# Attention in a diffusion step: rotary partners copied by DMA between partitions, the rotation on VectorE over 128 partitions one unit later

## The chip, the cores and the metric

One core of a Trainium2 chip runs the whole program. The metric is the device time of one execution in microseconds. TensorE (PE in the profile, its weight loads PEld) multiplies, VectorE (DVE), ScalarE (ACT) and GpSimd (POOL) do the elementwise work, and SyncE (SP) issues most of the DMA transfers. Each engine works through its own instructions one after the other.

## The reference

One inference step of a network of two layers over 128 context tokens and 512 latent tokens with 1024 features, in float32. Each layer has a SwiGLU block, a mixer, and a second SwiGLU block; the mixer of the first layer is a convolution with a gated unit, that of the second is attention. The change lies in that attention. Cut to what matters:

```
def rope_half(xp, ang):                       # xp: (..., 2F), cos and sin by position and feature
    a, b = xp[..., :F], xp[..., F:]
    return concatenate([a * cos - b * sin, b * cos + a * sin])

def axial_rope(x, ang_r, ang_c):              # 64 features of a head: 32 turn by the row, 32 by the column
    return concatenate([rope_half(x[..., :32], ang_r), rope_half(x[..., 32:], ang_c)])

qs, ks_, vs = split_qkv(hs @ attn_w_qkv[j])   # latent: 16 query heads, 4 key heads, 64 features each
qs, ks_ = axial_rope(qs, ...), axial_rope(ks_, ...)
ys = latent_attention(qs, ks_, vs, k_ctx, v_ctx, sink) @ attn_w_o[j]
```

The context tokens have attention of their own, without rotation. Latent queries see a window of 128 positions to either side and 128 cached context keys, with a learned sink in the softmax.

## The kernel before

**Layout.** Features lie on the 128 partitions, tokens along the free dimension: 128 context tokens and then 512 latent ones. All products are made in three float32r products of a high and a low part (`mm3`): a value is split into a high part, copied by ScalarE, and the rest, subtracted by VectorE. So each weight block costs a DMA, a ScalarE copy and a VectorE subtraction (`wload_ahead`, lines 184 to 213) before TensorE can use it, and so does each activation.

**The projections** (lines 1354 to 1392 and 1552 to 1555). Output block i of `wqkv` holds 128 features: blocks 0 to 7 are two query heads each, 8 and 9 two key heads each. A unit is one block for the 384 tokens of group GA or the 256 of GB: 24 matmuls in one PSUM bank, and an evacuation by ScalarE into `Q` (block i of the buffer `Y`) or `ks`. Blocks 0 to 3, 8 and 9 go in pairs for GA, with the making of `h` woven in; then GB of the keys and of blocks 0 to 3, and blocks 4 to 7 for both groups. `weights(i)` fetches a block where it is called, 4 to 7 within this run; buffers for raw weights are three, for split pairs six.

**The rotation** (`rope`, lines 1257 to 1272). The features are ordered so that a feature's partner lies 32 partitions away in the same 64. For a block of 512 latent tokens VectorE makes four products over 32 partitions each, partner times sine into a buffer `tmp` (four of these); POOL multiplies the block by the cosine in place over 128 partitions; VectorE adds. The sum is held back until the next rotation has begun (`last_rope`). Block 6 is taken otherwise: ScalarE copies the partners, and POOL makes both products. The keys go in two halves of 256 tokens, since 128 cached keys lie between them.

**The order.** Tensor, vector, scalar and POOL instructions are kept in the order of the code by a wrapper, `InOrder` (lines 61 to 78), and so all of them bear line 71 in the profile. DMAs on `nc.sync` are not wrapped; a planner places them. Keys and blocks 0 to 4 are rotated between the projections' units, each some units behind its evacuation. Between them lie `split_prompt` and `split_keys`, which split the keys for the scores, and the weights `wv` of the values (line 1387).

**The scores.** `prepare(t)` splits the 128 queries of token block t; t = 0 is the context, which isn't rotated. It can run when unit (7, GA) is evacuated. The first scores (`scores(0)`) follow unit (7, GB) on TensorE. The loop over m (lines 1571 to 1601) has eight steps per token block: scores two steps ahead, five pieces of value projection while m < 8, transposes of the probabilities, the exponentials, and six items of `leftover()`: the rotations of blocks 5 to 7 and `prepare(1)`, all during t = 0. Later `prepare(t)` casts on POOL.

Of the kernel before, what the change touches and what calls it, by code (L numbers as in the profile page):

```python
# [10 lines left out]
AF = mybir.ActivationFunctionType  # L11
ALU = mybir.AluOpType
AX = mybir.AxisListType

P = 128
# [5 lines left out]
NS = 512  # L21
# [68 lines left out]
class Builder:  # L90
# [1163 lines left out]
    def att_weight(self, i):  # L1254
        return ("qk", i), self.a["wqkv"][i], KC

    def rope(self, s, pos, on_act=False):


        nc, V = self.nc, self.nc.vector  # L1260
        t = self.tmp(pos.stop - pos.start)
        shaped = lambda u: u if len(s.shape) == 2 else u.rearrange("p (t q) -> p t q", q=P)
        sin, cos, t = (shaped(u) for u in (self.rsin[:, pos], self.rcos[:, pos], t))
        sides = [(slice(o, o + 32), slice(o ^ 32, (o ^ 32) + 32)) for o in range(0, P, 32)]
        first = [lambda: nc.pool.tensor_tensor(out=s, in0=s, in1=cos, op=ALU.mult)]

        if on_act:
            swap = [lambda r=r, q=q: nc.scalar.activation(out=t[r], in_=s[q], func=AF.Copy) for r, q in sides]
            first.append(lambda: nc.pool.tensor_tensor(out=t, in0=t, in1=sin, op=ALU.mult))
        else:  # L1270
            swap = [lambda r=r, q=q: V.tensor_tensor(out=t[r], in0=s[q], in1=sin[q], op=ALU.mult) for r, q in sides]
        return swap + first, lambda: V.tensor_tensor(out=s, in0=s, in1=t, op=ALU.subtract if on_act else ALU.add)

    def attention(self, h, lead, nxt, fetches):
        nc, a = self.nc, self.a
        V = nc.vector
        wts = {}
        Q = self.Y.rearrange("p (t i q) -> p t i q", i=KC, q=P)


        ks = [self.act() for _ in range(2)]
# [3 lines left out]
        def weights(i):  # L1285
            if i not in wts:
                wts[i] = self.take(*self.att_weight(i))
            return wts[i]

        def evac(ps, i, g):  # L1290
            if i < 8:
                nc.scalar.activation(out=Q[:, g[0] // P:g[1] // P, i, :], in_=ps.rearrange("p (t q) -> p t q", q=P),
                                     func=AF.Copy, scale=-0.125)
            elif g == GA:
                n = i - 8
                nc.scalar.activation(out=kpr[:, n * P:n * P + P], in_=ps[:, :P], func=AF.Copy)
                nc.scalar.activation(out=ks[n][:, 0:2 * P], in_=ps[:, P:], func=AF.Copy)
            else:
                nc.scalar.activation(out=ks[i - 8][:, 3 * P:], in_=ps, func=AF.Copy)

        def unit(i, g):
            evac(self.proj(weights(i), h, g), i, g)
# [2 lines left out]
            for ps, n in zip(self.proj2([weights(i), weights(j)], h, g, inserts), (i, j)):  # L1305
                evac(ps, n, g)

        last_rope = []

        def rope(s, pos, on_act=False):  # L1310

            ops = []

            def first():
                f, add = self.rope(s, pos, on_act)
                ops.extend(f)
                ops.pop(0)()
                last_rope.append(add)

            yield first  # L1320
            for _ in range(5 if on_act else 4):
                yield lambda: ops.pop(0)()
            yield lambda: last_rope.pop(0)() if len(last_rope) > 1 else None

        def rope_q(i, on_act=False):
            return rope(Q[:, 1:, i, :], slice(0, NS), on_act)

        def rope_k(n):
            return [f for half in range(2) for f in rope(ks[n][:, 3 * P * half:3 * P * half + 2 * P],
                                                         slice(2 * P * half, 2 * P * half + 2 * P))]  # L1330

        def run(*ops):
            for u in ops:
                for f in u:
                    f()
# [4 lines left out]
        def split_prompt():  # L1340
            for e in range(2):
                r = SIDE[e]
                for o in SIDE:
                    nc.scalar.activation(out=dup0[o, :, e, :], in_=pr(kpr[r]), func=AF.Copy)
                V.tensor_tensor(out=pr(kl0[r]), in0=pr(kpr[r]), in1=dup0[r, :, e, :].bitcast(F32), op=ALU.subtract)

        def split_keys(c):
            for e in range(2):
                r = SIDE[e]
                for o in SIDE:  # L1350
                    nc.scalar.activation(out=kst[2 * c + e][o], in_=ks[c][r], func=AF.Copy)
                V.tensor_tensor(out=kl[c][r], in0=ks[c][r], in1=kst[2 * c + e][r].bitcast(F32), op=ALU.subtract)
# [11 lines left out]
        kst = [self.act(F32R, lo=n % 2) for n in range(4)]  # L1364
        kl = [self.act(F32R, lo=True) for n in range(2)]
        weights(4)
        unit(0, GB)
        run(rope_k(0))
        unit(1, GB)
        weights(5)  # L1370
        run(rope_k(1))
        unit(2, GB)
        split_prompt()
        run(rope_q(0))
        unit(3, GB)
        weights(6)
        run(rope_q(1))
        unit(4, GA)
        split_keys(0)
        unit(4, GB)  # L1380
        weights(7)
        run(rope_q(2))
        unit(5, GA)
        split_keys(1)
        unit(5, GB)

        wv = [p for kk in range(2) for p in self.wload(a["wqkvv"][kk], 4, 256)]
        vs = self.vtok
        run(rope_q(3))
        unit(6, GA)  # L1390
        run(rope_q(4))
        unit(6, GB)

        def v_tile(t):

            ps = self.ps()
            for k in range(KC):
                yield lambda k=k: self.mm3(ps[:, :256], tuple(u[:, t * P:(t + 1) * P] for u in h[k]), wv[k],
                                           k == 0, k == KC - 1)
            yield lambda: nc.scalar.activation(out=vs[t], in_=ps[:, :256], func=AF.Copy)  # L1400
            if t == 0:
                nc.sync.dma_start(out=a["o_v"], in_=vs[0])
# [3 lines left out]
        qs, sc, st, pts, pos, op, ess, later = ({} for _ in range(8))  # L1406
# [9 lines left out]
        def prepare(t, engine=None):  # L1416

            qs[t] = self.wpair(D)
            st[t] = tuple(self.sm(16, n) for n in ("nmx", "ssum"))
            ops = [], []  # L1420
            for hf in range(2):
                q, *u = (u[:, hf * 512:hf * 512 + 512] for u in (self.y[t], *qs[t]))
                for r, o, v in zip(SIDE, SIDE[::-1], u):
                    if engine is None:
                        ops[0].append(lambda q=q, r=r, v=v: nc.scalar.activation(out=v[r], in_=q[r], func=AF.Copy))
                    else:
                        ops[0].append(lambda q=q, r=r, v=v: engine.tensor_copy(v[r], q[r]))
                    ops[1].append(lambda q=q, r=r, o=o, v=v: V.tensor_tensor(
                        out=v[o], in0=q[r], in1=v[r].bitcast(F32), op=ALU.subtract))
            return ops  # L1430
# [113 lines left out]
        load, parts = self.first_products(a["wo"], [0, 1], xsel, pieces=2, small=True)  # L1544
# [5 lines left out]
        n = len(steps)  # L1550
# [2 lines left out]
        up, low = prepare(0)  # L1553
        run(up, low)
        unit(7, GB)
        scores(0)()
        scores(1)()
        run(v_tile(0))

        def leftover():  # L1560

            for i in (5, 6, 7):
                yield from rope_q(i, i == 6)
            yield lambda: last_rope.pop(0)()
            up, low = prepare(1)
            yield from up
            yield from low
# [3 lines left out]
        for m in range(n + 4):  # L1571
            if m % 8 == 5 and m < n - 12:
                slow = [f for u in prepare(m // 8 + 2, nc.pool) for f in u]
            if m == n - 11:
                slow = load(0) + load(1)
            if m == n - 5:
                ops, res = self.wload_ahead(a["wo"][2], 2, 512, 2, True)
                wa.append(res)
                slow += ops
            if m == n - 1:  # L1580
                fill = parts
            exp = scores(m + 2) if m + 2 < n else None
            for _ in range(5 if m < 8 else 1):
                if fill:
                    fill.pop(0)()
            if m < n:
                transposes(m)
            if exp:
                exp()
            for _ in range(6):  # L1590
                next(extra, lambda: None)()
            if m != n - 11 and slow:
                slow.pop(0)()
            if 0 < m <= n and m % 2 == 0:
                for k, f in enumerate(values(m - 1)):
                    later.setdefault(m + (1, 2, 2, 3)[k], []).append(f)
            for f in later.pop(m, ()):
                f()
            if m == 8:
                while fill:  # L1600
                    fill.pop(0)()
# [371 lines left out]
```

## Time and profile before

| | |
|---|---|
| median of 3 runs | 2314.23 us (2311.72 to 2314.33) |
| the profiled execution | 2313.76 us |
| its span, first to last instruction | 2312.0 us |
| mean granted TensorE clock | 0.989 |
| busy: PE, PEld, DVE, ACT, POOL | 97%, 88%, 72%, 45%, 12% |
| rotation on POOL, 13 products | 1636.75 to 1702.6 us |
| scores begin | 1678.32 us |

All times are microseconds from the start of the span. A row of a timeline gives start, length, engine, line, operation, and the tile written and read, then the idle time of the engine before it and what ended that. The waits sum up such idle times: who waited for whom, how often, the longest. A group of instructions gives count, busy time and the mean in nanoseconds of one, then the idle time before them. A table by stage gives for each stretch the busy time of each engine, the granted clock (1.00 is full), the DMA share and GB/s.

### The profile page before, as it was taken

How to read it: one execution, taken by the hardware profiler on the slowest of the kernel's cores; microseconds unless marked ns; L12 is line 12 of the kernel's file. 1: busy time of each engine (PE TensorE's matmuls, PEld its weight loads, DVE VectorE, ACT ScalarE, POOL GpSimd, SP SyncE). 2: the span in 40 equal slices, each digit the busy share in tenths (PEclk: the TensorE clock that was granted, in tenths of full speed). 3: DMA queues.
4: the chain of work that ended last, by engine and by line, in shares of the span. 5: the costliest groups of instructions: out<-in, count | busy, mean ns of one | idle time of the engine just before them, and what ended most of it. 6: DMA issues, size and time to landing. Idle time of an engine off the chain costs nothing.

```text
span 2312.0 us, 35269 instructions
## 1 busy us (share of the span) xinstructions
PE 2253.7 (97%) x13692; PEld 2042.7 (88%) x13692; DVE 1658.4 (72%) x2758; ACT 1045.7 (45%) x1845; POOL 282.9 (12%) x377
## 2 busy tenths in 40 slices
PE   9999999999999999999998999999989999999998
PEld 7979898989889898989898989898866797989897
DVE  5688776877867786867777777786788678636366
ACT  5223343553165443434554434345558564434342
POOL 1000101021002111010011010102121021111100
PEclk9999999999999999999999999999989999999999
DMA  8564867542224577776636686864000345665644
GB/s 299 175 233 151 211 186 205 169 174 90 76 101 126 183 195 188 200 187 170 226 112 209 174 211 181 210 182 178 28 21 10 128 122 187 166 140 152 140 126 181
DMA packets 137672, 370.08 MB, mean 160 GB/s; under 512 B 14464, under 2 KB 16384, under 8 KB 136736
## 3 DMA queue, kind: packets, MB, share of 16 engines
q1 hardware_dynamic: 103952, 299.93, 38.0%
q0 software_dynamic: 33552, 67.90, 16.8%
q8 instruction: 107, 1.75, 0.3%
q14 instruction: 61, 0.50, 0.1%
HBM read 322.90 MB, written 42.25 MB: 158 GB/s over the span
## 4 chain that ended last, share of the span: by engine, by line
PE 71%; DVE 14%; DMA 6%; issue 5%; ACT 4%; POOL 1%; DVEq 0%; SPq 0%; ACTq 0%; POOLq 0%
PE ps L71 71%; DVE tmp L71 4%; DMA raw<-wmodT 4%; DVE scr L71 3%; DVE w L71 3%; ACT w L71 2%; DVE raw L71 1%; DMA rawx<-ws 1%; DVE act L71 1%; ACT tmp L71 1%; ACT act L71 1%; DVE Y L71 0%; ACT sum L71 0%; DVE sum L71 0%; DMA raw<-wu 0%
## 5 line engine op out<-in xcount | busy, mean ns | idle before, releaser
L71 PE MATMUL ps<-act,w 128*128 128x320 f32 (+6 forms) x6024 | 918.7, 320 | 25.2 <-DVE w L71 14.1
L71 PEld LDWEIGHTS ps<-act,w 128*128 128x128 f32 (+1 forms) x6024 | 849.2, 185 | 58.8 <-DVE w L71 18.7
L71 PE MATMUL ps<-w,act 128*128 128x512 f32 (+1 forms) x3480 | 785.3, 385 | 4.6 <-ACT tmp L71 3.1
L71 PEld LDWEIGHTS ps<-w,act 128*128 128x128 f32 x3480 | 627.0, 189 | 141.0 <-ACT tmp L71 3.5
L71 DVE TENSOR_TENSOR w<-raw,w 128x1024 fp32r<-128x1024 f32 (+1 forms) x340 | 410.7, 1220 | 205.3 <-ACT w L71 198.1
L71 PE MATMUL ps<-sum,w 128*128 128x320 f32 x3168 | 486.6, 312 | 14.4 <-ACT tmp L71 14.3
L71 PEld LDWEIGHTS ps<-sum,w 128*128 128x128 f32 x3168 | 474.2, 190 | 18.9 <-ACT tmp L71 18.9
L71 ACT ACTIVATE w<-raw 128x1024 fp32r<-128x1024 f32 (+1 forms) x340 | 350.6, 1047 | 194.8 <-DVE raw L71 97.5
L71 ACT ACTIVATE tmp<-ps 128x320 f32<-128x320 f32 (+4 forms) x450 | 209.4, 469 | 377.8 <-PE ps L71 310.2
L71 DVE CUSTOM_DVE_ANT_0 scr<-raw,cbc 128x1024 bf16<-128x1024 f32 x256 | 313.4, 1224 | 88.4 <-DMA raw<-wmodT 83.1
L71 ACT ACTIVATE act<-tmp 128x256 fp32r<-128x256 f32 (+4 forms) x238 | 114.8, 497 | 364.8 <-DVE tmp L71 364.7
L71 DVE TENSOR_TENSOR act<-tmp,act 128x256 fp32r<-128x256 f32 (+4 forms) x240 | 124.8, 528 | 116.9 <-ACT act L71 115.8
L911 POOL DMA_DIRECT2D ys<-tmp x120 | 91.3, 774 | 660.3 <-ACT tmp L71 650.5
L689 POOL DMA_DIRECT2D rawx<-ws x66 | 79.9, 1211 | 654.1 <-DMA rawx<-ws 194.4
L71 DVE TENSOR_TENSOR w<-rawx,w 128x1024 fp32r<-128x1024 f32 x66 | 80.8, 1224 | 28.7 <-ACT w L71 27.1
L71 DVE TENSOR_TENSOR tmp<-ps,tmp 128x320 f32<-128x320 f32 x132 | 64.0, 485 | 24.4 <-PE ps L71 21.4
L71 DVE TENSOR_TENSOR tmp<-tmp,tmp 128x640 f32<-128x640 f32 (+1 forms) x98 | 68.8, 715 | 6.4
L71 ACT ACTIVATE tmp<-ps,sh,G 128x256 f32<-128x256 f32 (+1 forms) x120 | 60.3, 525 | 22.7 <-PE ps L71 22.6
L71 ACT ACTIVATE w<-rawx 128x1024 fp32r<-128x1024 f32 x66 | 69.3, 1051 | 0.0
L71 DVE TENSOR_TENSOR tmp<-tmp,ps 128x320 f32<-128x320 f32 (+2 forms) x110 | 52.7, 479 | 18.0 <-ACT tmp L71 17.2
L71 ACT ACTIVATE tmp<-Y 128x1024 bf16<-128x1024 f32 (+2 forms) x39 | 35.1, 901 | 57.3 <-DVE Y L71 57.2
L71 ACT ACTIVATE Y<-X 128x1024 f32<-128x1024 f32 x30 | 31.8, 1058 | 54.7 <-DVE X L71 50.6
(165 smaller groups left out, 1281.9 us busy)
## 6 DMA issues: line engine op xcount, KB each, us to landing
raw<-wmodT SPq DMA_DIRECT2D x128, 512.0 KB, 4.7
raw<-ws SPq DMA_DIRECT2D x99, 512.0 KB, 4.7
raw<-wd SPq DMA_DIRECT2D x86, 512.0 KB, 4.1
rawx<-ws SPq DMA_DIRECT2D x66, 512.0 KB, 5.0
rawx<-ws POOLq DMA_DIRECT2D x66, 512.0 KB, 6.9
ys<-tmp POOLq DMA_DIRECT2D x120, 256.0 KB, 5.7
raw<-wg SPq DMA_DIRECT2D x22, 512.0 KB, 4.9
raw<-wu SPq DMA_DIRECT2D x22, 512.0 KB, 3.5
```

The lines of the kernel that those rows point to most:

```text
L71: i = method(*args, **kw)
L689: nc.gpsimd.dma_start(out=r.rearrange("p (a b) -> p a b", a=2), in_=w[:, 1536:2048].unsqueeze(1).to_broadcast([P, 2, 512]), accum_op=ALU.add)
L911: nc.gpsimd.dma_start(out=ys[t, half], in_=o, **(dict(accum_op=ALU.add) if pi else {}))
```

## The change

`rope` now takes all parts of a rotation at once and makes four DMAs per part, each copying 32 partitions from their partners into `tmp`, on SP's queue, at the place where it is called. It returns three VectorE instructions per part, over all 128 partitions: `tmp` by the sine, the block by the cosine, and their difference. POOL has no part in it, and block 6 is like the others. Each `rope_q(i)` is called behind the last unit of block i (the DMAs), and its instructions run a unit later; `split_prompt` moves ahead of unit (0, GB). Block 5 is rotated before the scores; blocks 6 and 7 stay in the loop, at three items a step in place of six.

```diff
-    def rope(self, s, pos, on_act=False):
+    def rope(self, parts):
...
-        sides = [(slice(o, o + 32), slice(o ^ 32, (o ^ 32) + 32)) for o in range(0, P, 32)]
-        first = [lambda: nc.pool.tensor_tensor(out=s, in0=s, in1=cos, op=ALU.mult)]
...
-            swap = [lambda r=r, q=q: V.tensor_tensor(out=t[r], in0=s[q], in1=sin[q], op=ALU.mult) for r, q in sides]
-        return swap + first, lambda: V.tensor_tensor(out=s, in0=s, in1=t, op=ALU.subtract if on_act else ALU.add)
+        whole = self.tmp(sum(pos.stop - pos.start for _, pos in parts))
+        ops, at = [], 0
+        for s, pos in parts:
...
+            for o in range(0, P, 32):
+                nc.sync.dma_start(out=t[o:o + 32], in_=s[o ^ 32:(o ^ 32) + 32])
+
+            ops += [lambda t=t, sin=sin: V.tensor_tensor(out=t, in0=t, in1=sin, op=ALU.mult),
+                    lambda s=s, cos=cos: V.tensor_tensor(out=s, in0=s, in1=cos, op=ALU.mult),
+                    lambda s=s, t=t: V.tensor_tensor(out=s, in0=s, in1=t, op=ALU.subtract)]
+        return ops
...
+        keys = [rope_k(n) for n in range(2)]
+        split_prompt()
         unit(0, GB)
-        run(rope_k(0))
+        q0 = rope_q(0)
+        run(keys[0])
         unit(1, GB)
         weights(5)
-        run(rope_k(1))
+        q1 = rope_q(1)
+        run(keys[1])
         unit(2, GB)
-        split_prompt()
-        run(rope_q(0))
+        run(q0)
+        q2 = rope_q(2)
         unit(3, GB)
         weights(6)
-        run(rope_q(1))
+        run(q1)
+        q3 = rope_q(3)
         unit(4, GA)
         split_keys(0)
         unit(4, GB)
         weights(7)
-        run(rope_q(2))
+        run(q2)
+        q4 = rope_q(4)
         unit(5, GA)
         split_keys(1)
         unit(5, GB)
+        q5 = rope_q(5)
 
         wv = [p for kk in range(2) for p in self.wload(a["wqkvv"][kk], 4, 256)]
         vs = self.vtok
-        run(rope_q(3))
+        run(q3)
         unit(6, GA)
-        run(rope_q(4))
+        run(q4)
         unit(6, GB)
+        q6 = rope_q(6)
+        run(q5)
...
         unit(7, GB)
+        q7 = rope_q(7)
...
-            for i in (5, 6, 7):
-                yield from rope_q(i, i == 6)
-            yield lambda: last_rope.pop(0)()
+            yield from q6
+            yield from q7
             up, low = prepare(1)
...
-            for _ in range(6):
+            for _ in range(3):
```

More of the change, by code (lines that the diff above doesn't have):

```diff
@@ L1255, in att_weight @@
         return ("qk", i), self.a["wqkv"][i], KC
-    def rope(self, s, pos, on_act=False):
+    def rope(self, parts):
         nc, V = self.nc, self.nc.vector
-        t = self.tmp(pos.stop - pos.start)
-        shaped = lambda u: u if len(s.shape) == 2 else u.rearrange("p (t q) -> p t q", q=P)
-        sin, cos, t = (shaped(u) for u in (self.rsin[:, pos], self.rcos[:, pos], t))
-        sides = [(slice(o, o + 32), slice(o ^ 32, (o ^ 32) + 32)) for o in range(0, P, 32)]
-        first = [lambda: nc.pool.tensor_tensor(out=s, in0=s, in1=cos, op=ALU.mult)]
[L1267 to L1270, printed above, removed]
-            swap = [lambda r=r, q=q: V.tensor_tensor(out=t[r], in0=s[q], in1=sin[q], op=ALU.mult) for r, q in sides]
-        return swap + first, lambda: V.tensor_tensor(out=s, in0=s, in1=t, op=ALU.subtract if on_act else ALU.add)
+        whole = self.tmp(sum(pos.stop - pos.start for _, pos in parts))
+        ops, at = [], 0
+        for s, pos in parts:
+            n = pos.stop - pos.start
+            shaped = lambda u: u if len(s.shape) == 2 else u.rearrange("p (t q) -> p t q", q=P)
+            sin, cos, t = (shaped(u) for u in (self.rsin[:, pos], self.rcos[:, pos], whole[:, at:at + n]))
+            at += n
+            for o in range(0, P, 32):
[4 more added lines that the diff above has]
+        return ops
     def attention(self, h, lead, nxt, fetches):
@@ L1306, in unit2, with rope_q @@
                 evac(ps, n, g)
[L1308 to L1326, printed above, removed]
+        def rope_q(i):
+            return self.rope([(Q[:, 1:, i, :], slice(0, NS))])
         def rope_k(n):
-            return [f for half in range(2) for f in rope(ks[n][:, 3 * P * half:3 * P * half + 2 * P],
-                                                         slice(2 * P * half, 2 * P * half + 2 * P))]
+            return self.rope([(ks[n][:, 3 * P * half:3 * P * half + 2 * P], slice(2 * P * half, 2 * P * half + 2 * P))
+                              for half in range(2)])
         def run(*ops):
```

## The prediction

> **What bounds the kernel now.** I read the page first, then the waits of TensorE, the timelines of each engine and tables by stage, for the attention stage alone, since the change touches nothing else.
>
> ```profile
> span 2312.0 us, 35269 instructions
> PE 2253.7 (97%) x13692; PEld 2042.7 (88%) x13692; DVE 1658.4 (72%) x2758; ACT 1045.7 (45%) x1845; POOL 282.9 (12%) x377
> ```
>
> TensorE bounds the whole: what isn't waited for by it is hidden. So the question is where it waits in the stretch from 1628 us (the first matmuls after the last of `h`) to 1715 us (token block t = 1 of the scores). The waits of TensorE there:
>
> ```profile
> PE ps L71 <- DVE w L71: 6.9, 2, 6.7
> PE ps L71 <- ACT tmp L71: 3.1, 2, 1.6
> PE ps L71 <- ACT raw L71: 0.8, 2, 0.6
> ```
>
> 10.8 us in six waits. From 1715 to 1860 us the same view has one wait of 0.2 us, so nothing is to be had there. Where they lie, from the tables by stage (stretch and length, PE, PEld, DVE, ACT, POOL busy, clock, DMA) and TensorE's timeline:
>
> ```profile
> 1633.55:1671.65 38.10, 38.10 (x277) 37.89 (x275) 37.17 (x51) 19.19 (x32) 8.40 (x8) 1.00 0.13 43
> 1671.65:1678.32 6.67, 0.00 (x0) 0.00 (x0) 6.52 (x8) 1.83 (x3) 3.29 (x2) 0.87 0.00 0
> 1678.32:1714.36 36.04, 31.79 (x190) 26.52 (x191) 26.33 (x66) 17.16 (x62) 9.09 (x8) 0.84 0.09 27
> ```
>
> ```profile
> 1684.00:1686.00 2.00, 2.00 (x12) 2.00 (x11) 0.00 (x0) 0.00 (x0) 0.00 (x0) 0.50 0.00 0
> ...
> 1708.00:1710.00 2.00, 2.00 (x9) 1.58 (x7) 1.61 (x7) 1.31 (x7) 0.00 (x0) 0.50 0.40 116
> ```
>
> ```profile
> 1678.32 0.47 PE L71 MATMUL ps<-act,w 128*128 128x128 f32 x1 [6.67 <-DVE w L71]
> 1679.04 1.90 PE L71 MATMUL ps<-act,w 128*128 128x128 f32 x7 [0.25 <-DVE w L71]
> 1680.87 5.49 PE L71 MATMUL ps<-w,act 128*128 128x256 f32 x24
> ...
> 1691.85 2.07 PE L71 MATMUL ps<-w,act 128*128 128x256 f32 x15
> ...
> 1706.49 1.68 PE L71 MATMUL ps<-w,act 128*128 128x256 f32 x9 [1.63 <-ACT tmp L71]
> ...
> 1709.10 1.60 PE L71 MATMUL ps<-act,w 128*128 128x384 f32 x4
> ...
> 1713.43 1.00 PE L71 MATMUL ps<-act,w 128*128 128x384 f32 x4
> ```
>
> Three losses. First, the projections end at 1671.65 us, and the scores can't start before 1678.32 us: their query halves `w` come from `prepare(0)`, whose VectorE part stands behind all that VectorE has still to do. VectorE is busy 37.17 of 38.10 us and then 6.52 of 6.67 us: it is the bound from 1633.55 to 1680 us. Second, the granted clock falls within that idle time (its mean is 0.87 there) and is still 0.50 at 1684 to 1686 us, 6 to 8 us after TensorE went on; at 1708 us, after more waits, it is 0.50 again. Third, the waits for ScalarE between 1694 and 1707 us (3.1 + 0.8 us), while ScalarE makes the swap copies of query block 6 and the casts of `prepare(1)`.
>
> **The change, part by part.** VectorE's work from 1633 to 1680.3 us, by groups (count, busy, mean ns):
>
> ```profile
> L71 DVE TENSOR_TENSOR tmp<-Y,ggrow 32x512 f32<-32x512 f32 x20 | 14.6, 731 | 0.3
> L71 DVE TENSOR_TENSOR w<-raw,w 128x1024 fp32r<-128x1024 f32 x6 | 8.7, 1471 | 4.1 <-ACT w L71 4.0
> L71 DVE TENSOR_TENSOR tmp<-act,ggrow 32x256 f32<-32x256 f32 x16 | 7.7, 480 | 0.3
> ...
> L71 DVE TENSOR_TENSOR Y<-Y,tmp 128x512 f32<-128x512 f32 x4 | 2.8, 692 | 0.1
> L71 DVE TENSOR_TENSOR act<-act,tmp 128x256 f32<-128x256 f32 x4 | 1.7, 424 | 0.1
> ```
>
> *VectorE's rotation.* A 32-partition product costs as much as a 128-partition one (a 512-element one 731 against 692 ns), so four quarter products go for one whole one. Out: 14.6 + 7.7 + 2.8 + 1.7 = 26.8 us. In: three instructions for each of four key halves (12 x 0.424 = 5.1 us) and for query blocks 0 to 5 (18 x 0.692 = 12.5 us; block 5 now lies ahead of `prepare(0)`): 17.6 us. Saved: 9.2 us ahead of the scores.
>
> *POOL's product.* It goes whole, and VectorE takes it over in the count above. Some of VectorE's instructions seem to be held beside it (the 32x512 products take 731 ns in the mean, the 128x512 sum 692). I put no price on that: what VectorE has to spare below does without it.
>
> *When VectorE is then done.* The order by hand is what decides, so I laid the new order on the old durations, with TensorE's pace unchanged. ScalarE's part:
>
> ```profile
> 1658.16 0.38 ACT L71 ACTIVATE Y<-ps 128x256 f32<-128x256 f32 x1
> 1658.57 2.01 ACT L71 ACTIVATE w<-raw 128x1024 fp32r<-128x1024 f32 x2
> ...
> 1668.84 0.49 ACT L71 ACTIVATE Y<-ps 128x384 f32<-128x384 f32 x1 [3.81 <-PE ps L71]
> 1669.23 2.58 ACT L71 ACTIVATE w<-Y 64x512 fp32r<-64x512 f32 x4
> ```
>
> ScalarE ends the two `wv` casts at 1660.6 us; VectorE's two lower halves of `wv` follow one cast behind (from 1659.6, 1.47 us each by the group) to 1662.5, blocks 3, 4 and 5 take 3 x 3 x 0.692 = 6.2 to 1668.7 us. `prepare(0)` can't begin before TensorE's unit (7, GA) is evacuated at 1669.3 us; a cast of 2.58 / 4 = 0.645 us and two lower halves (priced as the 512-element sum, 0.69 us) later (1671.3 us) the first scores have all they need. That is ahead of 1671.65: the wait of 6.67 us goes whole, and nothing of VectorE's is next; TensorE's own projections are. The margin is 1.2 us on VectorE, 0.3 us on ScalarE.
>
> *The copies.* They are new on SP's queue: 16 for the keys, 32 for the queries, each 32 partitions by 512 (or 256) floats, a query's in four runs of 512 bytes. The trace has near relatives, the copies between partitions of the convolution stage (start, length over all, count), and landing times (last column):
>
> ```profile
> 529.88 11.44 SPq L1050 DMA_DIRECT2D act<-Y  x16
> ...
> 550.82 5.65 SPq L1052 DMA_DIRECT2D act<-Y  x8
> ```
>
> ```profile
> act<-Y SPq DMA_DIRECT2D x24, 64.0 KB, 2.0
> ...
> raw<-wqkvv SPq DMA_DIRECT2D x2, 512.0 KB, 3.4
> ```
>
> So 5.65 / 8 = 0.71 us of SP each, and 2.0 us to land: a block's four are there 3 x 0.71 + 2.0 = 4.1 us after its evacuation. Block 5 is evacuated at 1658.5, lands at 1662.7, and is rotated from 1666.6 us; block 4 has more time. For the first key the second half lands about 1638.7 us (evacuated at 1632.2, behind some other copies), which holds VectorE some 2 us with the lower half of weights 5 queued behind it, done by 1641 us and needed by TensorE at 1650.5. Price: nothing, with the slack of VectorE as the cover.
>
> *What SP holds up.* In the code the weight loads 5, 6, 7 and `wv` now come behind copies that wait for evacuations. Whether that counts depends on whether SP keeps the code's order:
>
> ```profile
> 1640.87 12.06 SPq L196 DMA_DIRECT2D raw<-wqkvv  x2
> ```
>
> It doesn't seem to: the 16 copies of L1050 above went out in a row, though the code alternates them with those of L1052 as their targets are cleared. And loads went when a buffer of three came free: the two of `wv` at 1640.87 and some 12 us later, far ahead of their casts at 1658.57 us. I take it that they still do. The earlier `split_prompt` (four short casts at about 1633.5 us) only frees a `tmp` buffer; half a microsecond on an evacuation that nothing waits for.
>
> *The first score block.* With no idle time the clock should stay at 1.00. At half clock the 24 matmuls took 5.49 us; at the pace of the 15 in 2.07 they take 3.3 (2.2 less); the eight score matmuls before them, 0.47 + 1.90 us, can at most halve, I take 1.1 less: 3.3 us. The second fall: 9 matmuls in 1.68 against 1.24 (0.4), four scores 1.60 against 1.00 (0.6), and the turns and transposes between the two as much again, an estimate: 1.6 us. The waits left are 0.25 + 3.1 + 0.8 = 4.1 us. They came from four or five VectorE instructions, POOL's product and 2.5 us of ScalarE copies in a step of about 2.6 us; now a step has three VectorE instructions (2.07 us) or three casts (1.9 us) and no copies. I leave 1.5 us of waits (bounds 0 and 4.1; nearer the lower end, since the largest wait, 1.63 us, stood behind four casts at a stretch, and now it's three).
>
> *Sum.* 6.67 + 3.3 + 1.6 + 4.1 - 1.5 = 14.2 us. The profiled execution took 2313.76 us (its span and 1.76 around it), 0.47 under the median of the three runs: 2299.6 for such an execution, 2300.0 us for the median. All later stages just start earlier; the next waits of TensorE are theirs and unchanged.
>
> **The rivals.** *A, only `wv` late:* SP puts the two `wv` loads behind block 5's copies, as the code does. They go out at 1661.5 us behind the four copies, land 3.4 us on and, two at once, perhaps 5; the casts end at 1668.1, VectorE's lower halves at 1669.5, three blocks at 1675.7, the first lower half of `prepare(0)` at 1676.4: 1.9 of the 6.67 us are won, the clock falls as before, and after it 1.6 + 2.6 are won as above: 6.1 us, 2308.1. For: the code's order; against: the rows above. The clock is then the open point. By the Trainium skill's page TensorE: Matmul & The Clock Gate (Part 1), the clock drops after one idle window of about 3.4 us and comes back after as long a busy one; a wait of 4.7 us would still drop it, so by this rule too A keeps the loss. The trace agrees on the drop and not on the return, which took 6 us at least.
>
> *B, SP wholly in the code's order:* every load waits behind copies, and ScalarE, in order itself, stands at each cast. Load 5 goes out at 1643.7 and is cast by 1648.5, load 6 at 1652 and 1656.7, load 7's cast ends at 1661.5, block 5 is evacuated at 1665.3, `wv` lands by 1673.5; blocks 3 to 5 to 1682, the lower half to 1683. That is 5 us later than now, against 4.2 us won after it: 2315, no change.
>
> *C, copies one after the other:* if a copy's 2.0 us to landing don't overlap with the next one's, the 40 copies up to block 5 take 80 us from 1629.6 (the last `tmp` of `h` free) to 1709; rotation and lower half end 1712 instead of 1678.3: 33 us slower, 2347. It decides from (1674.9 - 1629.6) / 40 = 1.13 us a copy. Against: 0.71 us in the rows. By the Trainium skill's page DMA: Bandwidth & Descriptors (Rules for kernel authors), transfers to disjoint parts of the partitions "serialize", and under 64 KB one pays mostly overhead: a rule against this change. The trace agrees only in part, as eight went out in 5.65 us.
>
> **How the numbers follow.** Forecast 0.62, A 0.18, B 0.11, C 0.09. The forecast's own range is 2298.5 (no waits left) to 2304.2 (all 4.1 us of them and the second fall of the clock stay). With A the two hold 0.80, so the range goes to 2309 for A's unknowns and to 2297 below. Faster by over 0.2% (4.6 us, about what a measurement can tell from no change): forecast and A, 0.80; same: B, 0.11; slower: C, 0.09.
>
> **What would show it.** In the new profile: no wait of TensorE for VectorE's `w` near 1671 us, clock 1.00 from there to 1715, the 24 matmuls of the first value tile in 3.3 us; VectorE well under full from 1640 to 1670 us; the copies at about 0.7 us of SP each, landing in 2 us; the `wv` loads ahead of block 5's copies. The forecast is wrong if VectorE's idle time is put down to a copy (`tmp<-Y` or `tmp<-act`) close ahead of `prepare(0)`, if ScalarE waits for `raw`, or if waits for ScalarE after 1690 us keep their 4 us.

## The result, and the profile after

2297.95 us in the median of four runs (2296.32 to 2298.86), against 2313.71 us before (four runs, 2311.72 to 2314.33): a ratio of 0.9934, with a 95% interval of 0.9917 to 0.9950; the medians lie 15.8 us apart. The prediction was 2300.0 us.

The page and the waits of TensorE from 1628 to 1700 us, which answer to the 10.8 us in six waits of before:

```profile
span 2294.6 us, 35306 instructions
PE 2244.4 (98%) x13692; PEld 2037.1 (89%) x13692; DVE 1635.3 (71%) x2738; ACT 1042.9 (45%) x1841; POOL 263.7 (11%) x364
```

```profile
PE ps L71 <- ACT attc L71: 0.7, 1, 0.7
PE ps L71 <- DVE nmx L71: 0.2, 1, 0.2
```

The long wait for VectorE's `w` is gone. TensorE's timeline (start, length, and idle time before in brackets) has it in one piece: 332 matmuls from the projections of the keys through the first scores, then the first value tile, 3.14 us where it took 5.49, and four scores of t = 1 in 0.97 where they took 1.60.

```profile
1628.61 45.07 PE L71 MATMUL ps<-act,w 128*128 128x256 f32 x332
1673.61 3.14 PE L71 MATMUL ps<-w,act 128*128 128x256 f32 x24
...
1688.08 0.59 PE L71 MATMUL ps<-act,w 128*128 128x128 f32 x3 [0.68 <-ACT attc L71]
...
1694.09 0.97 PE L71 MATMUL ps<-act,w 128*128 128x384 f32 x4
```

The table by stage, for the 38.1 us up to the scores and for the score block (busy time of PE, PEld, DVE, ACT, POOL, then the clock, the DMA share and GB/s):

```profile
1634.50:1672.60 38.10, 38.10 (x279) 38.10 (x277) 28.82 (x45) 19.07 (x33) 0.00 (x0) 1.00 0.39 99
1672.60:1699.50 26.90, 26.05 (x195) 21.99 (x193) 18.70 (x62) 16.70 (x64) 2.85 (x4) 1.00 0.19 54
```

VectorE is busy 28.8 of 38.1 us where it was busy 37.2, and the clock is 1.00 throughout. How it got there, by VectorE's groups from 1634 to 1673.6 us:

```profile
L71 DVE TENSOR_TENSOR w<-raw,w 128x1024 fp32r<-128x1024 f32 x6 | 7.3, 1222 | 8.2 <-ACT w L71 8.1
L71 DVE TENSOR_TENSOR Y<-Y,tmp 128x512 f32<-128x512 f32 x6 | 4.2, 692 | 0.2
L71 DVE TENSOR_TENSOR tmp<-tmp,ggrow 128x512 f32<-128x512 f32 x6 | 4.1, 685 | 0.5 <-DMA tmp<-Y 0.5
L71 DVE TENSOR_TENSOR Y<-Y,ggrow 128x512 f32<-128x512 f32 x6 | 4.1, 684 | 0.0
...
L71 DVE TENSOR_TENSOR tmp<-tmp,ggrow 128x256 f32<-128x256 f32 x4 | 1.7, 422 | 1.1 <-DMA tmp<-act 1.1
```

The rotations take 12.4 us for six query blocks and 5.1 for the keys; all their waits for copies come to 1.6 us. And the lower halves of weights, which the change doesn't touch, are back at 1222 ns from 1471.

To compare runs, whose starts of this stage differ, I measure the stage from ScalarE's first evacuation of the keys' GB to the second turn of the softmax factors (`wide`). In the kernel before:

```profile
1631.84 0.74 ACT L71 ACTIVATE act<-ps 128x256 f32<-128x256 f32 x2 [2.73 <-PE ps L71]
...
1718.90 0.60 PE L71 MATMUL ps<-ident,wide 128*128 128x128 f32 x4
```

and after:

```profile
1632.82 0.74 ACT L71 ACTIVATE act<-ps 128x256 f32<-128x256 f32 x2 [2.75 <-PE ps L71]
...
1703.25 0.60 PE L71 MATMUL ps<-ident,wide 128*128 128x128 f32 x4
```

That is 87.1 and 70.4 us: 16.6 us less, the whole difference of the medians (15.8) and a little more. Whole times scatter more: single runs of the kernel before, beside the experiments, lie between 2303.57 and 2322.72 us. So differences of a few microseconds below are read from this stage and not from the times. Each kernel's stage is that of one traced execution; I read nothing from a tenth of a microsecond.

### The profile page after: what moved, and what is told of

It is laid out like the page before. It is cut to its first block, busy times and chain, and to the rows that moved or that the text cites. A ratio compares the mean times of both kernels' runs of the same rounds, so it can differ in the third digit from the quotient of the medians.

```text
span 2294.6 us, 35306 instructions
## 1 busy us (share of the span) xinstructions
PE 2244.4 (98%) x13692; PEld 2037.1 (89%) x13692; DVE 1635.3 (71%) x2738; ACT 1042.9 (45%) x1841; POOL 263.7 (11%) x364
## 4 chain that ended last, share of the span: by engine, by line
PE 69%; DVE 13%; DMA 7%; issue 5%; ACT 4%; POOL 1%; DVEq 0%; SPq 0%; ACTq 0%; POOLq 0%
PE ps L71 69%; DMA raw<-wmodT 4%; DVE scr L71 3%; DVE tmp L71 3%; DVE w L71 3%; DMA rawx<-ws 2%; ACT w L71 2%; ACT tmp L71 1%; DVE raw L71 1%; ACT act L71 1%; POOL nwq L71 1%; DVE Y L71 1%; DMA ys<-tmp 1%; DVE act L71 0%; ACT sum L71 0%
## 5 line engine op out<-in xcount | busy, mean ns | idle before, releaser
L71 ACT ACTIVATE tmp<-ps,sh,G 128x256 f32<-128x256 f32 (+1 forms) x120 | 60.3, 525 | 22.8 <-PE ps L71 22.7
L71 ACT ACTIVATE tmp<-Y 128x1024 bf16<-128x1024 f32 (+1 forms) x35 | 32.6, 932 | 57.5 <-DVE Y L71 57.5
```

What stands on the lines that cost most here:

```text
L71: i = method(*args, **kw)
```

## The experiments

| kernel | stage, us | median of its runs, us |
|---|---|---|
| before | 87.1 | 2313.71 |
| after | 70.4 | 2297.95 |
| before, cosine product on VectorE | 87.1 | 2309.84 |
| before, cosine product left out | 74.7 | 2301.76 |
| before, TensorE kept busy in the wait | 83.8 | 2313.04 |
| after, cosine product on POOL | 70.3 | 2296.10 |
| after, no rotation at all | 69.5 | 2300.14 |
| after, rotation at once | 70.4 | 2296.08 |
| after, copies on POOL's queue | 70.4 | 2293.87 |
| after, twice as many copies | 100.7 | 2327.42 |
| after, twice as many, on POOL's queue | 77.9 | 2306.48 |

My theory was that VectorE's time ahead of the scores was the bound, with the fall of the clock as its consequence, and that the copies hide. The rivals: that POOL's product was the cost; that the unit between copy and rotation is what makes it work; that SP's queue costs something.

**Is it POOL's product?** Twice in the kernel before, and once put back in the new one.

```diff
-        first = [lambda: nc.pool.tensor_tensor(out=s, in0=s, in1=cos, op=ALU.mult)]
+        first = [lambda: V.tensor_tensor(out=s, in0=s, in1=cos, op=ALU.mult)]
...
-            first.append(lambda: nc.pool.tensor_tensor(out=t, in0=t, in1=sin, op=ALU.mult))
+            first.append(lambda: V.tensor_tensor(out=t, in0=t, in1=sin, op=ALU.mult))
```

> The kernel before, with POOL's products of the rotation given to VectorE and nothing else changed. Theory (VectorE's instruction time ahead of the scores is the bound): VectorE gets 4 products of 0.42 and 5 of 0.69 us ahead of the scores, 5.1 us more, and is spared whatever POOL's products held up. In the trace of before, VectorE's instructions beside a POOL product are 0.4 us (keys) to 1.1 us (queries) longer, 5 to 6 us in all. The two cancel: the scores start within 1 us of 1678, and the loop is 0 to 2 us shorter: 2311 to 2315 us. Rival (VectorE isn't held by POOL, the longer instructions are chance): the scores start 5 us later, 2318 to 2321 us. Second rival (POOL's part in the chain was the cost, not VectorE's): over 6 us faster, under 2308.

The stage stayed at 87.1 us. TensorE's timeline, four of VectorE's groups, and the last of these as it was before the change:

```profile
1680.90 0.33 PE L71 MATMUL ps<-act,w 128*128 128x128 f32 x1 [3.84 <-DVE w L71]
...
1683.15 5.49 PE L71 MATMUL ps<-w,act 128*128 128x256 f32 x24
```

```profile
L71 DVE TENSOR_TENSOR tmp<-Y,ggrow 32x512 f32<-32x512 f32 x20 | 13.7, 683 | 0.3
L71 DVE TENSOR_TENSOR w<-raw,w 128x1024 fp32r<-128x1024 f32 x6 | 7.2, 1221 | 4.0 <-ACT w L71 4.0
L71 DVE TENSOR_TENSOR tmp<-act,ggrow 32x256 f32<-32x256 f32 x16 | 6.7, 417 | 0.3
...
L71 DVE TENSOR_TENSOR act<-act,act 64x640 fp32r<-64x640 f32 x4 | 3.3, 816 | 0.0
```

```profile
L71 DVE TENSOR_TENSOR act<-act,act 64x640 fp32r<-64x640 f32 x4 | 5.5, 1368 | 0.0
```

The keys' GB was evacuated at 1637.26 us in this run, so the scores start 43.6 us behind it, against 46.5 before: 2.8 us earlier, though VectorE has 5.1 us more to do. The groups say why: those that the edit doesn't touch are 7.2 us shorter in sum (the weights 1.5, the keys' lower halves 2.2, the quarter products 1.9, the lower halves of `prepare(0)` 1.0, those of `split_prompt` 0.6). So POOL's nine products had held VectorE up by 7 to 8 us, about as much as the quarter products cost it, and more than the 5 to 6 us that I expected. Giving them to VectorE wins nothing in the end: the wait of 3.84 us lets the clock fall all the same, and from the first value tile on the stage is longer, 41.2 us against 38.0, where I had expected a loop up to 2 us shorter. The products of blocks 5 to 7, now on VectorE's list in the loop, are the likely reason; that isn't tested apart. The median is 2309.84 us, a little under the expected 2311 to 2315, with a ratio of 0.9993 (0.9982 to 1.0003).

```diff
+        if not on_act:
+            first = [lambda: None]
         return swap + first, lambda: V.tensor_tensor(out=s, in0=s, in1=t, op=ALU.subtract if on_act else ALU.add)
```

> The kernel before with POOL's cosine product left out of all blocks but block 6 (so those are rotated wrongly): what POOL's product cost VectorE without being one of its instructions. Theory after the run with the product on VectorE (scores 2.8 us earlier though VectorE had 5.1 us more to do, so POOL's nine products held it 7.9 us): the scores wait less than 0.5 us, the clock stays, stage 72 to 76 us in place of 87.1. Rival (no hold; that run won in another way): 85 us or more.

The cosine product is left out here, of the keys and of all query blocks but block 6. 74.7 us, as expected; up to the first value tile TensorE's timeline shows no wait but 0.39 us, and a tile at full clock:

```profile
1673.20 1.21 PE L71 MATMUL ps<-act,w 128*128 128x128 f32 x7 [0.39 <-DVE w L71]
1674.34 3.11 PE L71 MATMUL ps<-w,act 128*128 128x256 f32 x24
...
1696.45 1.33 PE L71 MATMUL ps<-w,act 128*128 128x256 f32 x9 [1.18 <-ACT tmp L71]
...
1699.10 2.06 PE L71 MATMUL ps<-w,act 128*128 128x256 f32 x15
```

In the score block two waits for ScalarE are left, of 1.11 and 1.18 us, and behind the first the clock falls to 0.50, from about 1689 to 1692 us. So 12.4 of the 16.6 us come with the going of POOL's product alone, if nobody has to do its work. But its going isn't needed for the gain:

```diff
-            ops += [lambda t=t, sin=sin: V.tensor_tensor(out=t, in0=t, in1=sin, op=ALU.mult),
-                    lambda s=s, cos=cos: V.tensor_tensor(out=s, in0=s, in1=cos, op=ALU.mult),
+            ops += [lambda s=s, cos=cos: nc.pool.tensor_tensor(out=s, in0=s, in1=cos, op=ALU.mult),
+                    lambda t=t, sin=sin: V.tensor_tensor(out=t, in0=t, in1=sin, op=ALU.mult),
```

> The changed kernel, with the cosine product of each rotation back on POOL (issued ahead of VectorE's two); partners still come by DMA. Theory: VectorE saves 0.42 or 0.69 us a product and loses 0.4 to 1.1 us beside it, so its end ahead of the scores moves by 0 to 3 us; it has 1.1 us to spare in the trace after, so at most 2 us are lost and the clock stays at 1.00: 2298 to 2300 us. Rival (taking POOL out is where the gain came from): 5 us or more are lost, 2303 or more.

```profile
1668.55 1.21 PE L71 MATMUL ps<-act,w 128*128 128x128 f32 x7 [0.36 <-DVE w L71]
1669.69 3.14 PE L71 MATMUL ps<-w,act 128*128 128x256 f32 x24
```

70.3 us: VectorE ends late by 0.36 us ahead of the second score, and the loop gives it back. The hold is there in this run too (VectorE's sums `Y<-Y,tmp` take 1013 ns in the mean, against 692 after the change). What the change wins, it wins with or without POOL: quarter products and hold were both costs of VectorE, and either one's going took most of the long wait away.

**Is the clock a cost of its own?** TensorE multiplies unit (7, GB) twice more into unread banks while it would wait.

```diff
         unit(7, GB)
+        for _ in range(2):
+            self.proj(weights(7), h, GB)
         scores(0)()
```

> The kernel before, with unit (7, GB) multiplied twice more into banks that nothing reads (48 matmuls, 5.7 us of TensorE), in the 6.67 us in which TensorE waits for VectorE; the scores can't start earlier for it. Theory (the fall of the clock is a cost of its own, brought on by the idle time): the clock stays at 1.00 to the scores, the first value tile takes 3.1 to 3.3 us in place of 5.49, the scores before it about 1 us less: 3.3 us faster, 2310.4 us. Rival (the clock falls for another reason, or VectorE paces that stretch anyway): within 1 us of before, 2313 to 2315.

```profile
1682.35 0.30 PE L71 MATMUL ps<-act,w 128*128 128x128 f32 x1 [1.12 <-DVE w L71]
1683.07 1.18 PE L71 MATMUL ps<-act,w 128*128 128x128 f32 x7 [0.42 <-DVE w L71]
1684.17 3.11 PE L71 MATMUL ps<-w,act 128*128 128x256 f32 x24
```

The scores come 46.6 us behind the keys' evacuation as before, and the stage is 83.8 us: 3.3 us less, to the tenth what was priced. The median of its 12 runs (2313.04, ratio 1.000, interval 0.9985 to 1.0015) can't decide: the interval holds both the expected 2310.4 and the rival's 2313 to 2315. The stage alone tells them apart.

**Is anything left?** The changed kernel without copies and products (queries and keys aren't rotated):

> The changed kernel with the rotation left out: no copies, no products, so latent queries and keys aren't rotated. It bounds what is left to win. Theory (TensorE's own work is the bound of the whole stretch after the change, the rotation is hidden): 0.5 to 1 us less than the changed kernel, its two last waits: 2297 us. Rival (copies on SP or VectorE's instructions still cost something, say by holding load 7 back or by disturbing TensorE's pace): 3 us or more less, under 2295.

```diff
-        whole = self.tmp(sum(pos.stop - pos.start for _, pos in parts))
...
+        return []
```

69.5 us, 0.9 less than with the rotation. The only wait of TensorE left there is the one of 0.2 us for `nmx`, the same as in the kernel after. So the rotation now costs 0.9 us. (The median, 2300.14, is in the spread of the rest.)

**Is the unit between needed?** VectorE's instructions straight behind their copies, for query blocks 0 to 5:

```diff
         unit(0, GB)
-        q0 = rope_q(0)
         run(keys[0])
+        run(rope_q(0))
         unit(1, GB)
...
         unit(5, GB)
-        q5 = rope_q(5)
+        run(rope_q(5))
```

> The changed kernel, with VectorE's three instructions put straight behind their copies in the code, not a unit later (blocks 0 to 5; the keys as they are). The stage is read from the first evacuation of the keys' GB to the second turn of the softmax factors on TensorE: 87.1 us before, 70.4 after. Theory (VectorE has slack enough, each wait for a copy is paid from it): VectorE stands some 4 us for block 0's copies and 1 to 2 us for block 5's, the lower half of weights 6 is ready by 1656 and needed at 1658, weights 7 by 1661 and needed at 1666, and prepare(0) still waits for ScalarE: 70.4 us give or take 0.7. Rival (the unit between is what makes it work, VectorE's queue behind a waiting instruction holds TensorE up): 74 us or more.

70.4 us, no change. The waits of VectorE from 1629 to 1673 us in this kernel:

```profile
DVE w L71 <- ACT w L71: 6.0, 2, 4.0
DVE tmp L71 <- DMA tmp<-Y: 5.3, 3, 4.2
DVE tmp L71 <- DMA tmp<-act: 1.5, 1, 1.5
```

It does stand for the copies, 6.8 us against 1.6, and stands the less for ScalarE's casts, 6.0 us against 11.8. The unit of delay isn't where the gain lies: VectorE has to wait for ScalarE in any case.

**What do the copies cost?** They are not free on SP. Its queue after the change:

```profile
1629.39 10.78 SPq L1269 DMA_DIRECT2D tmp<-act  x16
1640.28 10.49 SPq L1269 DMA_DIRECT2D tmp<-Y  x16
1650.82 1.81 SPq L196 DMA_DIRECT2D raw<-wqkv  x1
1652.67 0.43 SPq L196 DMA_DIRECT2D raw<-wqkvv  x1
1653.21 2.59 SPq L1269 DMA_DIRECT2D tmp<-Y  x4
1655.89 0.54 SPq L196 DMA_DIRECT2D raw<-wqkvv  x1
1660.50 15.24 SPq L1269 DMA_DIRECT2D tmp<-Y  x12
```

0.66 us a copy. Weight load 7 went out at 1650.8, behind 32 copies, where it had gone at 1634.8 before; ScalarE stood 3.27 us for it:

```profile
1655.74 1.06 ACT L71 ACTIVATE w<-raw 128x1024 fp32r<-128x1024 f32 x1 [3.27 <-DMA raw<-wqkv]
```

Is that hidden, or a cost?

```diff
-                nc.sync.dma_start(out=t[o:o + 32], in_=s[o ^ 32:(o ^ 32) + 32])
+                nc.gpsimd.dma_start(out=t[o:o + 32], in_=s[o ^ 32:(o ^ 32) + 32])
```

> The changed kernel with its 48 copies issued on POOL's queue, so that SP's queue holds the weight loads alone again. Theory (SP's queue is late but hidden): load 7 goes out some 16 us earlier and ScalarE doesn't wait for it, which saves nothing; POOL issues a transfer in 0.6 to 0.9 us and they land in 5 to 7 us, so block 5 comes 4 us later than now, and VectorE's spare 1.1 us ahead of prepare(0) doesn't cover all of it: stage 70 to 73 us. Rival (the hold on load 7 costs something): under 69.8 us.

70.4 us: hidden. The load went early again, and nothing came of it in the stage. (The median of the four runs, 2293.87, is the lowest of all, but they lie between 2288.44 and 2300.92; I read nothing from it.) My price for POOL's queue was wrong on the good side: the queries' copies went out in about 0.54 us each and landed in 2.0, the keys' in 0.50 and 2.3, not 5 to 7:

```profile
tmp<-Y POOLq DMA_DIRECT2D x32, 64.0 KB, 2.0
```

Where the cover ends shows with twice the number, each copy of 16 partitions:

```diff
-            for o in range(0, P, 32):
-                nc.sync.dma_start(out=t[o:o + 32], in_=s[o ^ 32:(o ^ 32) + 32])
+            for o in range(0, P, 16):
+                nc.sync.dma_start(out=t[o:o + 16], in_=s[o ^ 32:(o ^ 32) + 16])
```

> The changed kernel with each copy of 32 partitions made as two of 16, so 96 in place of 48. Theory (SP issues some 0.66 us a copy whatever its size, and weight load 7 and those of the values stand behind the copies): the 64 copies of the keys and blocks 0 to 3 take 42 us of SP, load 7 goes out at 1672 in place of 1651, its lower half is ready at 1679 where TensorE needs it at 1666; with the values' loads and block 5 behind that the scores begin about 20 us later: a stage of 88 to 95 us, and a time of 2316 to 2322 us. Rival (copies are paid by their bytes, or SP has room): within 1 us of the changed kernel's 70.4.

100.7 us, 30 more than the changed kernel and worse than expected; 2327.42 us, ratio to before 1.0069 (1.0047 to 1.0090). Half the size saved SP nothing, 0.67 us a copy:

```profile
1650.10 21.57 SPq L1269 DMA_DIRECT2D tmp<-Y  x32
1671.71 0.58 SPq L196 DMA_DIRECT2D raw<-wqkv  x1
```

```profile
1661.16 8.50 PE L71 MATMUL ps<-act,w 128*128 128x384 f32 x46 [2.35 <-DVE w L71]
1676.52 1.01 PE L71 MATMUL ps<-act,w 128*128 128x384 f32 x2 [6.86 <-ACT w L71]
...
1698.48 0.47 PE L71 MATMUL ps<-act,w 128*128 128x128 f32 x1 [11.56 <-DVE w L71]
```

Load 7 went out at 1671.7 us (expected 1672), TensorE stood 6.86 us for its cast, and 11.56 for the scores, with block 5 and the values' weights behind it. I had missed the wait of 2.35 us and what the clock loses. To part the loads' lateness from the copies' own, the same on POOL's queue:

```diff
-                nc.sync.dma_start(out=t[o:o + 16], in_=s[o ^ 32:(o ^ 32) + 16])
+                nc.gpsimd.dma_start(out=t[o:o + 16], in_=s[o ^ 32:(o ^ 32) + 16])
```

> The kernel with 96 copies of 16 partitions, issued on POOL's queue in place of SP's: it parts what cost the 30 us of the run with half copies. Theory (it was mostly the weight loads held behind the copies on SP, less the copies' own lateness): loads go out early as with whole copies on POOL's queue; POOL issues a copy in 0.54 us, so the 32 of the keys take 17 us, the 32 of blocks 0 to 3 another 17, up to 1664 by the clock of the kernel after, block 4's eight go to 1668.5, block 5's to 1673, landing at 1675, 6 us after VectorE would want them; the scores start about 6 us late, the clock falls: stage 76 to 82 us in place of 100.7. Rival (the copies' lateness alone did it): 90 us or more. Rival (only the loads): 70.4.

```profile
1674.46 0.47 PE L71 MATMUL ps<-act,w 128*128 128x128 f32 x1 [3.84 <-DVE w L71]
1675.18 1.90 PE L71 MATMUL ps<-act,w 128*128 128x128 f32 x7 [0.24 <-DVE w L71]
1677.01 4.91 PE L71 MATMUL ps<-w,act 128*128 128x256 f32 x24
```

77.9 us: on POOL's queue the copies' own lateness costs 7.5 us, the clock's fall included. The other 22.8 us come with SP's queue, where loads stand behind copies. A copy also takes longer there, 0.67 us against some 0.5 on POOL's; how much of the 22.8 us that makes isn't parted.

## Why the prediction was right, and where it was off

*The wait of 6.67 us goes whole:* it did. From the keys' evacuation to the first value tile, before 49.0 us, after 40.8: 8.2 us less, against 6.67 + 0.25 + 1.1 predicted. VectorE ended block 5 at 1669.7 us; the prediction's 1668.7 was on a clock that ran 0.96 us ahead of this execution's. That the two meet to a tenth is luck: VectorE came to the lower halves of `wv` 1.0 us later than laid out, since load 7 had held ScalarE up, and then took 1.0 us less than laid out to the end of block 5. ScalarE's casts of `prepare(0)` then were the last to come, as laid out.

*Quarter products for whole ones, 9.2 us saved:* the new side was right (17.5 us for the rotations, 17.6 predicted). The old side of 26.8 us had part of POOL's hold in it: with no POOL product beside them the quarter products take 13.7 and 6.7 us in place of 14.6 and 7.7. So 7.3 us were theirs, and 1.9 belong to the next term.

*POOL's product, no price:* the weakest step. It was worth 7 to 8 us of VectorE's time ahead of the scores, about as much as the quarter products themselves. The weights' group with a mean of 1471 ns, for an instruction that takes 1222 without the hold, was in the table that the prediction quotes, and it used the long mean as the price of `wv`'s lower halves. It cost the forecast nothing, because TensorE's end at 1671.65 us cuts off what VectorE saves beyond the 6.9 us that TensorE waited for it; the run with the product back on POOL shows that.

*The clock stays at 1.00:* right, and the first fall measured by itself: 3.3 us predicted, 3.3 by the run that kept TensorE busy.

*The score block:* mis-sized. From the first value tile to the second turn the stage became 8.4 us shorter; the prediction's terms for that stretch (2.2 + 1.6 + 3.85 - 1.5) make 6.15. TensorE's rows say where the other 2.2 us lie. The waits left are 0.85 us, 0.17 of them in every kernel, where 1.5 was put: 0.85 us. The first fall of the clock took 2.6 us from the value tile on, not 2.2 (from its start to the next run of 15 matmuls 6.06 us before, 3.49 after). The second took 1.5 us, as priced: from the nine matmuls to the next run of 15 it is 4.14 us before (1706.49 to 1710.63) and 2.65 at full clock, in the run without the cosine product. The last 1.1 us lie around the waits, where a run broken by a wait loses more than the wait: twelve matmuls in two pieces take 1.80 us besides their wait of 1.47, from 1695.69 us before, and 1.53 in one piece after. Which of the loop's changes took the waits away (block 5 ahead of it, no copies by ScalarE, no POOL) no run parts.

*SP's order:* half right. The planner put the loads of `wv` ahead of block 5's copies, so rival A didn't come; but load 7 went behind 32 copies, which is rival B in small. So one of the prediction's signs of being wrong did come, ScalarE waiting for `raw` (3.27 us). Its price was hidden, as copies on POOL's queue showed, and the cover is thin: with twice the copies on SP the loss is 30 us.

*Rival C* (copies in series): they cost 0.66 us each and land in 2.0 while the next go out. Its threshold of 1.13 us a copy isn't tested apart: at 1.34 us of SP for the same 32 partitions the kernel was slower than before, but mostly by what SP's queue did to the rest; at some 1.0 us of POOL's queue the stage was still 9.1 us shorter than before.

## What to carry to other kernels

When one engine's queue ends in the instruction that the bottleneck waits for, everything in that queue has a price, and so has what another engine does to it; look for one instruction form with two durations before pricing anything. Savings beyond the point where the next engine is late buy nothing, so lay the new order on the old durations and find that point first. Many small copies are paid in issue time of their queue, and the weight loads that share it pay too.

## What the runs showed of the hardware

- POOL products of two SBUF operands held VectorE's `tensor_tensor` instructions up by some 7 us in all over nine products (the keys' lower halves 1368 against 816 ns). By the Trainium skill's page SBUF — State Buffer (Terms), the port pair that the two share is an exclusive lock and the loser "fully blocks". The kernel before agrees: VectorE's `nmx`, 0.16 us elsewhere, takes 0.80 us beside a POOL product and ends as that ends, at 1702.6 us. The nine products kept POOL busy for longer than the hold, 4 x 0.84 + 5 x 1.64 = 11.6 us; the shortest took 0.74 and 1.27 us, so part of that may be POOL's own waiting.

```profile
1701.33 1.27 POOL L71 TENSOR_TENSOR Y<-Y,ggrow 128x512 f32<-128x512 f32 x1
1701.82 0.80 DVE L71 TENSOR_TENSOR nmx<-mx,ggrow 128x1 f32<-128x1 f32 x1
```

- The clock fell after a wait of 3.84 us too, and only when TensorE was back at work: in the kernel before with the cosine on VectorE it was 1.00 until 1682 us, 5 us behind the start of the gap, and then 0.50 to about 1689, as these rows show (last columns: clock, DMA share, GB/s). Shorter waits did it too: in the run without the cosine product the clock fell to 0.50 behind a wait of 1.11 us.

```profile
1680.00:1682.00 2.00, 0.71 (x4) 0.50 (x4) 1.91 (x4) 0.00 (x0) 0.00 (x0) 1.00 0.00 0
1682.00:1684.00 2.00, 2.00 (x10) 1.70 (x11) 1.89 (x7) 0.57 (x3) 0.00 (x0) 0.54 0.00 0
```

- A copy between partitions takes some 0.66 us of SP whether it moves 16, 32 or 64 KB, and 0.48 to 0.54 us of POOL; on either queue it landed in about 2 us (medians 1.8 to 2.3).
